# A four-layer decoder trunk on one core: weight-quarter sums spread over three layers, two more raw weight buffers and later transposes in the last layer

## The chip, the cores and the metric

The kernel runs on one core of a Trainium2 chip as one launch. The metric is the device time of that launch in microseconds (us). Each kernel is timed several times and the median is compared; the kernel before takes 844.87 us (three runs, 844.37 to 845.11).

## What is computed

Four residual layers work on x, 256 positions by 1024 channels, in float32. Layers 0 and 3 are gated MLPs with a spatial mix over chunks of 128 positions (mixer A), layer 1 is dilated-window attention (mixer B), layer 2 is causal pooling (mixer C).

```python
for i in range(DEPTH):                      # 4 layers: A, B, C, A
    h = rms_norm(x, norm_gain[i])
    x = x + mixer[i](h, ...)

def mixer_a(h, w_in, v_gain, w_s, b_s, w_out):
    proj = h @ w_in                          # 1024 x 6144
    u, v, z = proj[..., :2048], rms_norm(proj[..., 2048:4096], v_gain), proj[..., 4096:]
    mixed = einsum('gij,bcjgd->bcigd', tril(w_s), v) + b_s
    return (u * mixed * silu(z)) @ w_out     # 2048 x 1024
```

## The kernel before

**Weights as a stream.** All weights lie in DRAM as 272 units of 128 x 1024 float32 (512 KB each) in the order of their use. A unit is loaded by the SP queue into a raw buffer (tile wr, four buffers, `RAW_BUFS`), then split in two parts that the matmul takes exactly: ScalarE copies the high part (w..h, L85), VectorE subtracts to get the low part (w..l, L88). When the low part of unit u is made, the raw buffer is free and the load of unit u+4 may start. Seven pairs of split tiles exist (`W_BUFS`); a unit is split about five units before TensorE uses it (`AHEAD`). A product is three matmuls, high by high, high by low, low by high (`mm3`, L80 to L82). In most projections a unit feeds 12 matmuls with 512 columns.

**The order of the work.** The program is written by generators. A projection calls `tick()` twice per unit; each tick runs the tasks that are due (activation work, transposes, splits). `yield n` means: go on n ticks later. So the numbers in `yield` set the order of the instructions on every engine, and each engine runs its own instructions strictly in that order. SP, which issues the loads, does too: a load that has to wait holds up all loads behind it.

**The seven products.** In layer 3, the column blocks n = 1 and n = 3 of z and u are computed with seven block products in place of eight (`seven_products`, L651 to L716 of the kernel before). They need sums of weight quarters. Those sums are made during earlier layers by `sums_of_quarters` (L158): 16 rounds, each of which loads four quarters into the one tile qs (tag "xs", L167), adds four times on VectorE (L170, 128 x 256 each), and stores the result to DRAM (sums, L172). The next round's load must wait until the store has read qs. Each product unit then feeds only 6 matmuls, so units are used up twice as fast as elsewhere: 14 units in one block.

**Transposes of y.** In layers 0 and 3 a task (`y_task`, L595) multiplies u, the mixed v and the gate into yy on VectorE, then transposes yy in two halves on TensorE (yp, L620), makes high and low parts, and frees the one PSUM bank "tr" for the second half. In layer 1 the same bank takes the transposes of q and k (qt, L815), whose low parts are made at L823.

Of the kernel before, what the change touches and what calls it, by code (L numbers as in the profile page):

```python
# [10 lines left out]
F32 = mybir.dt.float32  # L11
# [6 lines left out]
P = 128  # L18
# [3 lines left out]
HALF = 512  # L22
# [15 lines left out]
RAW_BUFS = 4  # L38
# [5 lines left out]
LAST_AHEAD = 3  # L44
WARM = 13
SEVEN = (1, 3)
FIRST_PARTS = 5


@with_exitstack  # L50
def hybrid_trunk_kernel(ctx, tc, x, wts, norm_gainT, a_v_gain, a_wsT, a_bsT, b_gl, b_gv, c_scaleT,
                        masks, rope, rcnt, out):
    nc = tc.nc
    n_units = wts.shape[0]
# [42 lines left out]
    def spawn(gen, delay=0):  # L97
        if delay == 0:
            try:
                delay = next(gen)  # L100
            except StopIteration:
                return
        tasks.append([now[0] + delay, gen])
# [26 lines left out]
    used = [0]  # L130
    loaded = [0]
    split = [0]

# [11 lines left out]
                        for j in range(2)]  # L147
    n_seq = len(seq)

    def load_units(n):  # L150
        while loaded[0] < min(n, n_seq):
            i = loaded[0]
            raw = wp.tile([P, 2, HALF], F32, tag="wr", name=f"wr{i}", bufs=RAW_BUFS)
            src = sums[seq[i][0], seq[i][2]][seq[i][1]] if isinstance(seq[i], tuple) else wts[seq[i]]
            nc.sync.dma_start(raw, src.rearrange("p (k n) -> p k n", n=HALF))
            raws.append(raw)
            loaded[0] += 1

    def sums_of_quarters(parts):

        for n, j, c in parts:
            z = seven_units(n) + j
            cs = slice(c * 256, (c + 1) * 256)
            q = cp.tile([P, 4, 256], F32, tag="xs", name=f"qs{n}{j}{c}", bufs=1)
            nc.sync.dma_start(q, wts[z:z + 8:2][:, :, cs].rearrange("i p c -> p i c"))  # L167
            yield 6
            for a, b in ((0, 2), (2, 3), (3, 0), (1, 3)):
                nc.vector.tensor_tensor(q[:, a], q[:, a], q[:, b], op=ALU.add)  # L170
            yield 3
            nc.sync.dma_start(sums[n, j][:, :, cs].rearrange("i p c -> p i c"), q)  # L172
            yield 4

    lowered = [0]

    def split_hi(n):

# [8 lines left out]
    def split_units(n):  # L187

        split_hi(n)
        while lowered[0] < min(n, n_seq):  # L190
            u = lowered[0]
            lo_of(units[u][1], raws[u], units[u][0])
            lowered[0] += 1
            load_units(u + 1 + RAW_BUFS)

    def next_unit():

# [27 lines left out]


    raws.append(wp.tile([P, 2, HALF], F32, tag="wr", name="wr0", bufs=RAW_BUFS))
    loaded[0] += 1
    first_unit = wts[0].rearrange("p (k n) -> p k n", n=HALF)
    nc.scalar.dma_start(raws[0][:, 0], first_unit[:, 0])  # L230
# [20 lines left out]
    def h_parts(layer):  # L251

        o = 16 if layer in (0, DEPTH - 1) else 0
        return [hT[:, o + i * KT * S:o + (i + 1) * KT * S].rearrange("p (k s) -> p k s", s=S) for i in range(2)]
# [99 lines left out]
    def proj_first(name):  # L354

        o = [pp(f"{name}_{t}") for t in range(2)]
        pts = {}
        hh, hl = h_parts(0)

        def turn(u):  # L360
            pts[u] = (trp if u == 3 else atp)(f"hp0{u}").rearrange("p (k t c) -> p k t c", t=2, c=P)
            for t in range(2):
                for k in range(2):
                    nc.tensor.transpose(pts[u][:, k, t], xt[t][:, (2 * u + k) * P:(2 * u + k + 1) * P], ident)

        def part(k):
            return pts[k // 2][:, k % 2].rearrange("p t c -> p (t c)"), gT[:, 0, k:k + 1]

        def high(k):
            pt, g = part(k)  # L370
            nc.scalar.activation(hh[:, k], pt, AF.Copy, scale=g)

        def low(k):
            pt, g = part(k)
            nc.vector.scalar_tensor_tensor(hl[:, k], pt, g, hh[:, k].bitcast(F32), op0=ALU.mult, op1=ALU.subtract)

        def w_pair(u):
            units.append(pair(wp, [P, 2, HALF], "w", f"w{u}", W_BUFS))
            split[0] += 1

        def w_high(u, kk):
            hi_of(units[u][0][:, kk], raws[u][:, kk])

        def w_low(u, kk):
            lo_of(units[u][1][:, kk], raws[u][:, kk], units[u][0][:, kk])
            if kk:
                lowered[0] += 1
                load_units(u + 1 + RAW_BUFS)

        def products(k):  # L390

            wh, wl = (a[:, k % 2] for a in units[k // 2])
            for t in range(2):
                for i, h in enumerate(h_t(k, t)):
                    nc.tensor.matmul(o[t], h, wh, start=k == 0 and i == 0, stop=False, skip_group_check=True)
            for t in range(2):
                nc.tensor.matmul(o[t], h_t(k, t)[0], wl, start=False, stop=k == KT - 1, skip_group_check=True)

        turn(0)
        turn(1)  # L400
        w_pair(0)
        high(0)
        high(1)
        low(0)
        low(1)
        for kk in range(2):
            w_high(0, kk)
            w_low(0, kk)
        products(0)
        products(1)  # L410
        turn(2)
        high(2)
        high(3)
        low(2)
        low(3)
        w_pair(1)
        for kk in range(2):
            w_high(1, kk)
            w_low(1, kk)
        products(2)  # L420
        high(4)
        high(5)
        split_hi(3)
        low(4)
        low(5)
        split_units(3)
        products(3)
        turn(3)
        split_hi(4)
        split_units(4)  # L430
        products(4)
        high(6)
        high(7)
        low(6)
        low(7)
        for k in range(5, KT):
            products(k)
        used[0] += 4
        split_units(5)
        for t in range(2):  # L440
            ss = tiny(2, f"ss_{t}")
            for n in range(2):
                half_ss(t, n, ss)
            norm_rms(0, t, ss)
        split_units(6)
        for t in range(2):
            done.add(("h", 0, t))
        for _ in range(8):
            tick()
        return o  # L450
# [74 lines left out]

    def layer_a(layer, consts, pl, mid):
        hcur[:] = h_parts(layer)
        first = proj_first(f"v{layer}0") if layer == 0 else None
        kc, wsT, bsT = consts()

# [64 lines left out]
                mxs[n].append(mx)  # L595
            done.add(("mx", layer, n))

        def y_task(n, up, us):
            while ("mx", layer, n) not in done:
                yield 1  # L600
            yh, yl = pair(pl, [P, 4, S], "v", f"y{layer}{n}", 5)
            yT.append((yh, yl))
            ys = []
            for t in range(2):
                y = tmp("yy", f"yy{layer}{n}{t}", 2)
                if late(layer):
                    nc.vector.scalar_tensor_tensor(us[t], up[t], r_tok[t][:, 0:1], us[t], op0=ALU.mult, op1=ALU.mult)  # L607
                else:
                    nc.vector.tensor_tensor(us[t], up[t], us[t], op=ALU.mult)
                for gg in range(2):  # L610
                    sl = slice(gg * 256, (gg + 1) * 256)
                    nc.vector.scalar_tensor_tensor(y[:, sl], mxs[n][t][:, sl], bsT[:, 2 * n + gg:2 * n + gg + 1],  # L612
                                                   us[t][:, sl], op0=ALU.add, op1=ALU.mult)
                ys.append(y)
            yield 2
            for t in range(2):
                sl = slice(t * P, (t + 1) * P)
                pt = trp(f"yp{layer}{n}{t}").rearrange("p (k c) -> p k c", c=P)
                for k in range(4):
                    nc.tensor.transpose(pt[:, k], ys[t][:, k * P:(k + 1) * P], ident)  # L620
                hi_of(yh[:, :, sl], pt)
                yield 1
                lo_of(yl[:, :, sl], pt, yh[:, :, sl])
                if t == 0:
                    yield 1
            done.add(("y", layer, n))
# [24 lines left out]
        def seven_products(n):  # L651
# [41 lines left out]
            z0, u0 = r["p1"], r["n2"]  # L693
# [19 lines left out]
                yield 1  # L713

            spawn(second_task(), 1)
            spawn(y_task(n, (u0, u1), (z0, z1)), 2)  # L716

        for n in range(4):
            spawn(v_task(n, first if first and n == 0 else
# [1 line left out]
            if layer == DEPTH - 1 and n == 0:  # L721
                spawn(sums_task(), 4)
        if layer == 0:
            spawn(sums_of_quarters(parts[:FIRST_PARTS]))
        for n in range(4):
            if layer == DEPTH - 1 and n in SEVEN:
                seven_products(n)
# [39 lines left out]
    def layer_b(layer, consts, pl):  # L767
# [215 lines left out]
        for hp in range(NHEAD // 2):  # L983
            for g in range(NG):
                spawn(qk_task(hp, g, proj_tok(f"qk{hp}{g}", skew=layer if hp == 0 and g == 0 else None)))
                if hp == 0 and g == 0:
                    spawn(sums_of_quarters(parts[FIRST_PARTS:]))
                    gate(0)
                    gate(1)
            o = proj_tok(f"v01{hp}")  # L990
# [24 lines left out]
    def layer_c(layer, pl):  # L1015
# [103 lines left out]

        a, b, c, d = C_ORDER  # L1120
        spawn(gate_tok(a, proj_tok(f"cz{a}", skew=layer)))
        spawn(gate_feat(b, proj_feat(f"cz{b}")))
        spawn(pool_task(a, proj_feat(f"cx{a}")))
        spawn(pool_task(b, proj_feat(f"cx{b}")))
# [170 lines left out]
```

## Time and profile before

| | us |
|---|---|
| median of the timed runs | 844.87 |
| the profiled execution | 843.5 |
| its span on the engines | 841.7 |
| TensorE (PE) busy | 827.1 (98%) |
| VectorE (DVE) busy | 593.8 (71%) |
| ScalarE (ACT) busy | 508.5 (60%) |
| GpSimd (POOL) busy | 42.0 (5%) |

The profiled execution lies 1.4 us below the median, and the span 1.8 us below its own time. TensorE is busy nearly all the time, so what a change can win is mostly the time in which TensorE stands still, and the time in which its clock is not granted in full. Times in the rows are microseconds from the span's start. Layer 0 ends near 195 us, layer 1 near 494, layer 2 near 651.

### The profile page before, as it was taken

The page shows a single profiled execution, that of the slowest core. Times are in us where ns is not written, and L with a number is a line of the kernel's source. Part 1 is how long each engine was busy: PE and PEld are TensorE (multiplying, and loading weights), DVE is VectorE, ACT ScalarE, POOL GpSimd, SP SyncE. Part 2 cuts the span into 40 slices and gives each one's busy share as a digit, 9 for nine tenths or more (in the row PEclk, how much of TensorE's full clock was granted, in tenths as well). Part 3 has the DMA queues.
Part 4 walks back from the last instruction along what each step waited for, and adds up shares of the span by engine and source line. Part 5 has one row for each costly group of instructions (what it writes and reads, how often), then busy time and mean ns, then how long its engine had stood idle before and what let it go on. Part 6 is the DMA issues. An engine that isn't in the chain of part 4 may idle for free.

```text
span 841.7 us, 12513 instructions
## 1 busy us (share of the span) xinstructions
PE 827.1 (98%) x4565; PEld 713.0 (85%) x4565; DVE 593.8 (71%) x1006; ACT 508.5 (60%) x937; POOL 42.0 (5%) x69
## 2 busy tenths in 40 slices
PE   8998999999999999999999999999999999999998
PEld 7887888888988888888888889999988888778786
DVE  5876667546858678678668576798754898786861
ACT  7764444336768687687687567446543676565640
POOL 1101000000000010010010011000000000000000
PEclk9999999999999999999999999999999999999999
DMA  8878776662877556557566267547664467676851
GB/s 288 292 245 264 226 222 210 222 196 82 290 254 227 172 173 219 185 163 234 179 192 209 76 224 255 175 151 243 200 210 151 138 211 242 214 263 200 280 176 51
DMA packets 60654, 172.66 MB, mean 205 GB/s; under 512 B 5584, under 2 KB 22496, under 8 KB 60464
## 3 DMA queue, kind: packets, MB, share of 16 engines
q1 hardware_dynamic: 59328, 167.79, 60.6%
q0 software_dynamic: 976, 3.79, 1.4%
q8 instruction: 36, 0.59, 0.3%
q10 hardware_dynamic: 288, 0.28, 0.2%
q14 instruction: 26, 0.21, 0.1%
HBM read 162.40 MB, written 9.44 MB: 204 GB/s over the span
## 4 chain that ended last, share of the span: by engine, by line
PE 83%; DVE 7%; DMA 5%; ACT 3%; issue 2%; POOL 0%; DVEq 0%; SPq 0%; ACTq 0%
PE wo L80 6%; PE wo L82 6%; PE wo L81 6%; PE v L82 5%; PE v L80 5%; PE v L81 5%; PE qk L82 4%; PE qk L80 4%; PE qk L81 4%; PE u L81 2%; PE u L80 2%; PE u L82 2%; PE cz L81 2%; PE cz L80 2%; PE cz L82 2%
## 5 line engine op out<-in xcount | busy, mean ns | idle before, releaser
L790 POOL TENSOR_TENSOR qr<-qm,m 128x8 f32<-128x8 f32 x12 | 19.7, 1638 | 230.5 <-DVE qm L789 230.5
L785 ACT ACTIVATE junk<-qk 128x128 bf16<-128x128 f32 x96 | 26.6, 277 | 7.2 <-PE qk L82 4.5
L794 ACT ACTIVATE qn<-qk,qr 128x128 f32<-128x128 f32 x96 | 27.5, 380 | 3.4 <-POOL qr L790 3.4
L170 DVE TENSOR_TENSOR qs<-qs 128x256 f32<-128x256 f32 x64 | 27.1, 424 | 2.5 <-DMA qs<-in_wts_dram 0.9
L496 DVE TENSOR_TENSOR x<-wo,x 128x512 f32<-128x512 f32 x16 | 11.0, 689 | 20.1 <-PE wo L82 20.0
L292 ACT ACTIVATE hT<-hp,gT 128x128 fp32r<-128x128 f32 x48 | 13.0, 383 | 14.9 <-PE hp L288 14.9
L785 ACT ACTIVATION_READ_ACCUMULATOR junk<-qk 128x1 f32 x96 | 18.9, 197 | 0.0
L297 DVE SCALAR_TENSOR_TENSOR hT<-hp,gT,hT 128x128 fp32r<-128x128 f32 x48 | 13.5, 343 | 7.4 <-ACT hT L292 7.4
L274 POOL TENSOR_TENSOR r<-ms,m 128x1 f32<-128x1 f32 x6 | 4.3, 708 | 277.3 <-DVE ms L271 277.3
L789 DVE TENSOR_SCALAR qm<-qs 128x8 f32<-128x8 f32 x12 | 2.1, 172 | 22.1 <-ACT junk L785 22.1
L266 ACT ACTIVATE junk<-x 128x512 bf16<-128x512 f32 x16 | 10.2, 640 | 9.6 <-DVE x L496 9.4
L815 PE MATMUL qt<-ident,qn 128*128 128x128 f32 x96 | 14.5, 273 | 1.4 <-DVE qk10l L823 0.6
L815 PEld LDWEIGHTS qt<-ident,qn 128*128 128x128 f32 x96 | 11.3, 140 | 4.9 <-issue 2.2
L884 ACT ACTIVATE p<-p,rl 128x384 f32<-128x384 f32 (+1 forms) x16 | 11.5, 769 | 5.0 <-DVE rl L883 5.0
L620 PE MATMUL yp<-ident,yy 128*128 128x128 f32 x64 | 10.3, 285 | 4.0 <-DVE y00l L88 2.5
L620 PEld LDWEIGHTS yp<-ident,yy 128*128 128x128 f32 x64 | 7.9, 144 | 7.2 <-DVE y00l L88 2.9
L545 DVE TENSOR_TENSOR vv<-v,kc 128x512 f32<-128x512 f32 x16 | 10.7, 686 | 4.5 <-ACT junk L543 4.2
L807 DVE TENSOR_TENSOR rb<-qn,kcb 128x32 f32<-128x32 f32 x96 | 13.8, 185 | 0.0
L607 DVE SCALAR_TENSOR_TENSOR sz<-u,m,sz 128x512 f32<-128x512 f32 x8 | 6.0, 746 | 10.1 <-PE u L82 10.1
L880 ACT ACTIVATE p<-p,nb 128x768 f32<-128x768 f32 x8 | 7.5, 938 | 8.9 <-DVE nb L879 8.9
L803 DVE TENSOR_TENSOR ra<-qn,kcb 128x64 f32<-128x64 f32 x48 | 10.6, 221 | 1.0 <-ACT qn L794 0.4
L612 DVE SCALAR_TENSOR_TENSOR yy<-mx,bs,sz 128x256 f32<-128x256 f32 x24 | 10.5, 480 | 0.4
(2887 smaller groups left out, 3309.3 us busy)
## 6 DMA issues: line engine op xcount, KB each, us to landing
wr<-in_wts_dram SPq DMA_DIRECT2D x267, 512.0 KB, 4.4
qs<-in_wts_dram SPq DMA_DIRECT2D x16, 512.0 KB, 5.5
sums<-qs SPq DMA_DIRECT2D x16, 512.0 KB, 5.1
wr<-sums SPq DMA_DIRECT2D x16, 512.0 KB, 4.7
kc<-in_a_wsT_dram POOLq DMA_DIRECT2D x2, 512.0 KB, 7.4
kc<-in_a_v_gain_dram POOLq DMA_DIRECT2D x1, 1024.0 KB, 5.2
out_dram<-x SPq DMA_DIRECT2D x4, 256.0 KB, 2.0
kc<-in_a_v_gain_dram POOLq DMA_DIRECT2D x1, 768.0 KB, 6.6
```

What stands on the lines that cost most here:

```text
L80: nc.tensor.matmul(out_ap, lh[0], rh[0], start=start, stop=False, skip_group_check=True)
L81: nc.tensor.matmul(out_ap, lh[0], rh[1], start=False, stop=False, skip_group_check=True)
L82: nc.tensor.matmul(out_ap, lh[1], rh[0], start=False, stop=stop, skip_group_check=True)
L170: nc.vector.tensor_tensor(q[:, a], q[:, a], q[:, b], op=ALU.add)
L292: nc.scalar.activation(h_parts(layer)[0][:, k, t * P:(t + 1) * P], pt[:, k % 4], AF.Copy, scale=gT[:, layer, k:k + 1])
L297: nc.vector.scalar_tensor_tensor(hTl, pt[:, k % 4], gT[:, layer, k:k + 1], hTh.bitcast(F32), op0=ALU.mult, op1=ALU.subtract)
L620: nc.tensor.transpose(pt[:, k], ys[t][:, k * P:(k + 1) * P], ident)
L785: nc.scalar.activation(junk[:, :HD], ov[t][:, h], AF.Square, accum_out=ssq[t][:, h:h + 1])
L790: nc.gpsimd.tensor_tensor(rqs, ms, m05_row[:, :8], op=ALU.pow)
L794: nc.scalar.activation(qn[t][:, h], ov[t][:, h], AF.Copy, scale=rq[t][:, h:h + 1])
L807: nc.vector.tensor_tensor(rb[:, hs, s0:s0 + 16], qn[t][:, hs, s1:s1 + 16], c, op=ALU.mult)
L815: nc.tensor.transpose(pts[t][:, h], qn[t][:, h], ident)
```

## The change

The first group of rounds of quarter sums is 4 instead of 5, in layer 0; the second is 8 instead of 11, in layer 1; the remaining 4 rounds are moved to layer 2. Inside a round, the adds begin seven ticks after the load instead of six, and the four adds are one tick apart instead of together.

In layer 3, from unit 224 of the sequence on (the first unit of z), raw units go round six buffers instead of four: the four of wr, the tile xs, which the rounds no longer need by then, and a new tile wx in the layer's own pool. A load starts when the buffer it goes to is free.

In the two blocks with seven products, `y_task` waits five ticks instead of two before it transposes.

```diff
-FIRST_PARTS = 5
+PARTS = (4, 8)
...
+    raw_users = {"wr": [-1] * RAW_BUFS, "xs": [-1], "wx": [-1]}
+    last_pool = [None]
+
+    def raw_place(i):
+
+        return ("wr", "wr", "wr", "wr", "xs", "wx")[i % 6] if i >= n_units - 48 else "wr"
+
+    def load_free():
+
+        while loaded[0] < n_seq and raw_users[raw_place(loaded[0])][0] < lowered[0]:
+            load_units(loaded[0] + 1)
+
     def load_units(n):
         while loaded[0] < min(n, n_seq):
             i = loaded[0]
-            raw = wp.tile([P, 2, HALF], F32, tag="wr", name=f"wr{i}", bufs=RAW_BUFS)
+            tag = raw_place(i)
+            pool = {"wr": wp, "xs": cp, "wx": last_pool[0]}[tag]
+            raw = pool.tile([P, 2, HALF], F32, tag=tag, name=f"wr{i}", bufs=len(raw_users[tag]))
+            raw_users[tag] = raw_users[tag][1:] + [i]
...
-            yield 6
+            yield 7
             for a, b in ((0, 2), (2, 3), (3, 0), (1, 3)):
                 nc.vector.tensor_tensor(q[:, a], q[:, a], q[:, b], op=ALU.add)
-            yield 3
+                yield 1
+            yield 2
...
             lowered[0] += 1
-            load_units(u + 1 + RAW_BUFS)
+            load_free()
...
-            yield 2
+            yield wait
             for t in range(2):
                 sl = slice(t * P, (t + 1) * P)
                 pt = trp(f"yp{layer}{n}{t}").rearrange("p (k c) -> p k c", c=P)
...
-            spawn(y_task(n, (u0, u1), (z0, z1)), 2)
+            spawn(y_task(n, (u0, u1), (z0, z1), 5), 2)
...
-            spawn(sums_of_quarters(parts[:FIRST_PARTS]))
+            spawn(sums_of_quarters(parts[:PARTS[0]]))
...
-                    spawn(sums_of_quarters(parts[FIRST_PARTS:]))
+                    spawn(sums_of_quarters(parts[PARTS[0]:sum(PARTS)]))
...
         spawn(gate_tok(a, proj_tok(f"cz{a}", skew=layer)))
+        spawn(sums_of_quarters(parts[sum(PARTS):]))
```

The order on VectorE in layer 0, in the first half of the first transposed block y00; qs are the adds of a round, w29l to w32l low parts of weights. Before:

```order
62 L612 SCALAR_TENSOR_TENSOR yy_765<-mx_711,bs_254,sz_666 128x256 x2
63 L88 TENSOR_TENSOR w29l<-wr_687,w29h 128x1024
64 L170 TENSOR_TENSOR qs_727<-qs_727 128x256 x4
65 L88 TENSOR_TENSOR y00l<-yp_786,y00h 128x4x128
66 L88 TENSOR_TENSOR w30l<-wr_719,w30h 128x1024
67 L88 TENSOR_TENSOR y00l<-yp_815,y00h 128x4x128
68 L88 TENSOR_TENSOR w31l<-wr_739,w31h 128x1024
```

The same place after the change:

```order
63 L629 SCALAR_TENSOR_TENSOR yy_763<-mx_710,bs_254,sz_664 128x256 x2
64 L88 TENSOR_TENSOR w29l<-wr_686,w29h 128x1024
65 L88 TENSOR_TENSOR y00l<-yp_786,y00h 128x4x128
66 L88 TENSOR_TENSOR w30l<-wr_718,w30h 128x1024
67 L88 TENSOR_TENSOR y00l<-yp_811,y00h 128x4x128
68 L88 TENSOR_TENSOR w31l<-wr_737,w31h 128x1024
69 L186 TENSOR_TENSOR qs_775<-qs_775 128x256
70 L88 TENSOR_TENSOR w32l<-wr_755,w32h 128x1024
```

The four adds that stood ahead of both y00l now stand behind them.

The order on VectorE in layer 1, third pair of heads, from the low part of unit 117 to that of q and k (qk20l); qn is the rotation. Before:

```order
350 L808 TENSOR_TENSOR qn_3563<-ra_3655,rb_3656 128x4x32
351 L88 TENSOR_TENSOR w119l<-wr_3501,w119h 128x1024
352 L823 SCALAR_TENSOR_TENSOR qk20l<-qt_3682,gv,qk20h 128x2x128 x2
353 L88 TENSOR_TENSOR w120l<-wr_3556,w120h 128x1024
354 L170 TENSOR_TENSOR qs_3615<-qs_3615 128x256 x4
```

The same place after; two more adds stand further ahead, one between szT and yb1l and one behind w118l:

```order
367 L825 TENSOR_TENSOR qn_3544<-ra_3636,rb_3637 128x4x32
368 L186 TENSOR_TENSOR qs_3443<-qs_3443 128x256
369 L88 TENSOR_TENSOR w119l<-wr_3483,w119h 128x1024
370 L186 TENSOR_TENSOR qs_3443<-qs_3443 128x256
371 L840 SCALAR_TENSOR_TENSOR qk20l<-qt_3665,gv,qk20h 128x2x128 x2
372 L88 TENSOR_TENSOR w120l<-wr_3537,w120h 128x1024
```

Here four adds that stood behind qk20l now stand ahead of it.

The order on VectorE in layer 3 behind the first block of seven products; yy is the product that is transposed, y31l its low part. Before:

```order
759 L612 SCALAR_TENSOR_TENSOR yy_7777<-mx_7714,bs_5173,n_7734 128x256 x2
760 L88 TENSOR_TENSOR w251l<-wr_7695,w251h 128x1024
761 L88 TENSOR_TENSOR w252l<-wr_7722,w252h 128x1024
762 L88 TENSOR_TENSOR y31l<-yp_7799,y31h 128x4x128
763 L88 TENSOR_TENSOR w253l<-wr_7737,w253h 128x1024
764 L88 TENSOR_TENSOR y31l<-yp_7824,y31h 128x4x128
```

The same place after:

```order
793 L629 SCALAR_TENSOR_TENSOR yy_7781<-mx_7718,bs_5145,n_7738 128x256 x2
794 L88 TENSOR_TENSOR w251l<-wr_7673,w251h 128x1024
795 L88 TENSOR_TENSOR w252l<-wr_7685,w252h 128x1024
796 L88 TENSOR_TENSOR w253l<-wr_7699,w253h 128x1024
797 L88 TENSOR_TENSOR y31l<-yp_7830,y31h 128x4x128
798 L88 TENSOR_TENSOR w254l<-wr_7726,w254h 128x1024
799 L88 TENSOR_TENSOR y31l<-yp_7861,y31h 128x4x128
```

Each y31l stands one unit later here. On TensorE both transposes of y31 (and of y33 in the second block) stand a unit and a half further back: the first, which stood behind unit 247, is now in the middle of unit 249, the second in the middle of unit 250. On SP, the units before 224 are loaded in the same order as before between the rounds' loads and stores.

## Rows read from the trace of the kernel before

**Rows 1.** The page's list of engines: busy time, share of the span, instructions.

```profile
PE 827.1 (98%) x4565; PEld 713.0 (85%) x4565; DVE 593.8 (71%) x1006; ACT 508.5 (60%) x937; POOL 42.0 (5%) x69
```

**Rows 2.** The view of waits, TensorE alone: line, what it waited for, us in total, times, longest.

```profile
PE xb L80 <- ACT n L668: 2.5, 2, 1.5
PE yp L620 <- DVE y00l L88: 2.5, 1, 2.5
...
PE yp L620 <- DVE y31l L88: 1.1, 1, 1.1
...
PE yp L620 <- DVE y33l L88: 0.3, 1, 0.3
...
PE wo L80 <- DVE n L711: 0.3, 1, 0.3
```

**Rows 3.** The view of windows in layer 0: stretch, its length, busy us (instructions) of PE, PEld, DVE, ACT, POOL, then the granted clock, the share of the DMA engines and GB/s.

```profile
80.00:84.00 4.00, 1.58 (x7) 0.95 (x6) 3.30 (x7) 0.41 (x1) 0.00 (x0) 1.00 0.87 310
84.00:88.00 4.00, 3.91 (x13) 3.30 (x14) 3.04 (x5) 2.49 (x3) 0.00 (x0) 0.57 0.49 115
```

**Rows 4.** The timeline of TensorE there: start, us, engine, line, operation, in brackets idle time before and who ended it.

```profile
80.97 0.39 PE L81 MATMUL z<-w25l,hT 128*128 128x512 f32 x1
81.19 0.39 PE L82 MATMUL z<-w25h,hT 128*128 128x512 f32 x1
84.09 1.11 PE L620 MATMUL yp<-ident,yy 128*128 128x128 f32 x4 [2.51 <-DVE y00l L88]
...
85.43 0.63 PE L81 MATMUL z<-w26l,hT 128*128 128x512 f32 x1
85.86 0.63 PE L82 MATMUL z<-w26h,hT 128*128 128x512 f32 x1
```

**Rows 5.** The timeline of VectorE there.

```profile
79.82 1.21 DVE L88 TENSOR_TENSOR w29l<-wr,w29h 128x1024 fp32r<-128x1024 f32 x1
81.63 1.81 DVE L170 TENSOR_TENSOR qs<-qs 128x256 f32<-128x256 f32 x4 [0.60 <-DMA qs<-in_wts_dram]
83.35 0.68 DVE L88 TENSOR_TENSOR y00l<-yp,y00h 128x512 fp32r<-128x512 f32 x1
```

**Rows 6.** The timelines of SP's queue and of ScalarE there: the store of the first round, the load of the second, and the high part of unit 28.

```profile
66.66 0.43 SPq L172 DMA_DIRECT2D sums<-qs  x1
...
75.66 0.38 SPq L167 DMA_DIRECT2D qs<-in_wts_dram  x1
...
74.44 1.06 ACT L85 ACTIVATE w28h<-wr 128x1024 fp32r<-128x1024 f32 x1 [6.19 <-DMA wr<-in_wts_dram]
```

**Rows 7.** The timelines of VectorE and TensorE in layer 1, second pair of heads.

```profile
304.54 1.79 DVE L170 TENSOR_TENSOR qs<-qs 128x256 f32<-128x256 f32 x4
...
307.39 0.87 DVE L823 SCALAR_TENSOR_TENSOR qk10l<-qt,gv,qk10h 128x256 fp32r<-128x256 f32 x2
...
308.41 0.63 PE L815 MATMUL qt<-ident,qn 128*128 128x128 f32 x4 [0.56 <-DVE qk10l L823]
```

**Rows 8.** The same in the third pair of heads.

```profile
364.04 0.42 DVE L88 TENSOR_TENSOR yb1l<-szT,yb1h 128x256 fp32r<-128x256 f32 x1 [0.48 <-ACT yb1h L85]
...
369.61 0.88 DVE L823 SCALAR_TENSOR_TENSOR qk20l<-qt,gv,qk20h 128x256 fp32r<-128x256 f32 x2 [0.23 <-ACT qk20h L817]
...
371.29 0.60 PE L815 MATMUL qt<-ident,qn 128*128 128x128 f32 x4
```

**Rows 9.** The timeline of ScalarE in the two blocks of seven products.

```profile
734.65 1.06 ACT L85 ACTIVATE w245h<-wr 128x1024 fp32r<-128x1024 f32 x1 [0.17 <-DMA wr<-sums]
735.62 0.58 ACT L668 ACTIVATE n<-xb 128x512 f32<-128x512 f32 x1
...
783.47 1.06 ACT L85 ACTIVATE w267h<-wr 128x1024 fp32r<-128x1024 f32 x1 [0.20 <-DMA wr<-sums]
784.44 0.58 ACT L668 ACTIVATE n<-xb 128x512 f32<-128x512 f32 x1
```

**Rows 10.** The timeline of VectorE in the same blocks.

```profile
725.97 1.22 DVE L88 TENSOR_TENSOR w239l<-wr,w239h 128x1024 fp32r<-128x1024 f32 x1
...
774.21 1.22 DVE L88 TENSOR_TENSOR w261l<-wr,w261h 128x1024 fp32r<-128x1024 f32 x1
...
795.24 0.69 DVE L711 TENSOR_TENSOR n<-wb,n 128x512 f32<-128x512 f32 x1
```

**Rows 11.** The view of windows, columns as in rows 3: a stretch of layer 0 in which loads run one behind the other, one just before a block of seven products, and the first part of each block.

```profile
69.00:75.00 6.00, 6.00 (x32) 5.12 (x31) 0.75 (x1) 0.56 (x1) 0.00 (x0) 1.00 0.98 352
...
718.00:724.00 6.00, 6.00 (x30) 4.97 (x30) 3.86 (x7) 2.22 (x3) 0.00 (x0) 1.00 0.16 58
724.00:736.00 12.00, 11.28 (x52) 8.97 (x50) 10.00 (x11) 9.57 (x12) 0.00 (x0) 1.00 0.83 261
...
772.00:785.00 13.00, 11.52 (x54) 9.18 (x52) 10.40 (x11) 9.72 (x12) 0.00 (x0) 1.00 0.80 260
```

**Rows 12.** Layer 2: a window, and from the timelines the low part of unit 179 and the first matmul that uses it.

```profile
540.00:560.00 20.00, 20.00 (x177) 20.00 (x176) 19.73 (x31) 8.92 (x13) 0.38 (x3) 1.00 0.49 158
...
568.03 1.22 DVE L88 TENSOR_TENSOR w179l<-wr,w179h 128x1024 fp32r<-128x1024 f32 x1
...
572.58 0.28 PE L82 MATMUL cg<-cd2h,w179l 128*128 128x256 f32 x1
```

**Rows 13.** The page's list of DMA issues: KB each, median us from issue to landing.

```profile
wr<-in_wts_dram SPq DMA_DIRECT2D x267, 512.0 KB, 4.4
```

More of the change, by code (lines that the diff above doesn't have):

```diff
@@ L132, in hybrid_trunk_kernel @@
     split = [0]
+    lowered = [0]
     seq = list(range(n_units))
@@ L167, in sums_of_quarters @@
             nc.sync.dma_start(q, wts[z:z + 8:2][:, :, cs].rearrange("i p c -> p i c"))
-            yield 6
+            yield 7
             for a, b in ((0, 2), (2, 3), (3, 0), (1, 3)):
                 nc.vector.tensor_tensor(q[:, a], q[:, a], q[:, b], op=ALU.add)
-            yield 3
+                yield 1
+            yield 2
             nc.sync.dma_start(sums[n, j][:, :, cs].rearrange("i p c -> p i c"), q)
             yield 4
-    lowered = [0]
     def split_hi(n):
@@ L227, in hybrid_trunk_kernel @@
     raws.append(wp.tile([P, 2, HALF], F32, tag="wr", name="wr0", bufs=RAW_BUFS))
+    raw_users["wr"] = raw_users["wr"][1:] + [0]
     loaded[0] += 1
@@ L387, in w_low @@
                 lowered[0] += 1
-                load_units(u + 1 + RAW_BUFS)
+                load_free()
         def products(k):
@@ L527, in layer_a @@
         hcur[:] = h_parts(layer)
+        last_pool[0] = pl
         first = proj_first(f"v{layer}0") if layer == 0 else None
@@ L596, in mix_task, with y_task @@
             done.add(("mx", layer, n))
-        def y_task(n, up, us):
+        def y_task(n, up, us, wait=2):
             while ("mx", layer, n) not in done:
```

## The prediction

> **What bounds the kernel now.** I read the page's list of engines first: TensorE is busy for 827.1 of 841.7 us [rows 1], so the span can only shrink by TensorE's idle time and by time at a lower clock. Then I read TensorE's own waits [rows 2]; the reader should see that they are few and that each has a place. One wait of 2.5 us is for y00l, in layer 0. Two that add up to 2.5 us are for a ScalarE copy of xb, one in each block of seven products. y31l costs 1.1 us, y33l and L711 0.3 us each, all in layer 3. Third I read the windows around the first wait for the clock [rows 3]: from 80 to 84 us TensorE works 1.58 us at a granted clock of 1.00, and from 84 to 88 us the mean is 0.57. Last come the timelines of the engine that is waited for.
>
> A wait costs a little more than its idle time. From 81.19 to 84.09 two instructions start 2.90 us apart, where 0.22 us is the normal step from 80.97 to 81.19 [rows 4]: 2.68 us lost for 2.51 us listed idle, so I add 0.17 us per wait.
>
> **Layer 0: first round later, second round behind y00l.** The clock fell right behind the 2.51 us of idle time. Steps are 0.43 us from 85.43 to 85.86 in place of 0.22 [rows 4], which is 1.2 in place of 2.4 GHz, and a mean of 0.57 over 4 us is 1.7 us lost [rows 3]. With the pipeline's own overlap I count 1.5 us of that, so this place costs 2.7 + 1.5 = 4.2 us. Its cause is on VectorE [rows 5]: w29l is done at 81.0, the four adds then wait 0.60 us for their data and take 1.81 us, and y00l follows at 83.35. The data is late because the load of round two could not be issued before 75.66, when the store issued at 66.66 had been read out [rows 6]. In the new order the adds are behind both y00l. Without them y00l would start at 81.0 and end at 81.7, while TensorE wants the bank at 81.4: 0.3 us would be left. That rest should go too, since the store now stands behind two more weight loads on SP, which therefore start before it; unit 28, for which ScalarE stood still 6.19 us until 74.44 [rows 6], should land earlier, and with it everything that VectorE does up to w29l. Some 0.3 us earlier is enough. I take -4.2 us; the bounds are -3.8 (0.3 us left, no fall of the clock) and -4.2. What is late next there is nothing that TensorE waits for: the adds of round two come behind w31l, and weights there are split more than 5 us before use.
>
> **Layer 1: eight rounds, adds in ones and twos.** An add takes 0.45 us (1.81 for four [rows 5]). What matters is how many stand between a transpose and the low part that frees the bank. In the second pair of heads, four adds at 304.54 stand ahead of qk10l and TensorE waits 0.56 us [rows 7]; now three do, so -0.4 us. In the third pair, four adds that stood behind qk20l are now ahead of it (the order above). The first falls into an idle 0.48 us of VectorE [rows 8]; three remain, 1.35 us, less the 0.23 us for which VectorE idles before qk20l: 1.1 us later. qk20l ended at 370.49 and TensorE passed at 371.29 without a wait, with the 0.15 us that lie between the end of qk10l and the transpose that waited for it [rows 7]: slack of 0.65 us, so +0.4 us. In the other pairs as many adds stand ahead as before, or they fall where VectorE idles. The sum is 0. Bounds: -2.2 us if all waits of layer 1 went (the 0.56 us [rows 7] and the smaller ones of its kind), +2 us if three pairs were hit like the third and with no slack. The waits of up to 1.5 us did not lower the clock in this trace; the one of 2.5 us did [rows 2, 3].
>
> **Layer 2: four rounds added.** Sixteen adds of 0.45 us, 7.2 us of VectorE, beside a TensorE that never waits there; four loads and four stores on SP and the DMA engines, which are at 0.49 in the busiest stretch for VectorE [rows 12]. That stretch is the place to look at: VectorE is busy 19.73 of 20 us, and one round's 1.8 us is pushed on to the next idle time. The least slack behind it is unit 179: low part done at 569.25, first used at 572.58, 3.3 us [rows 12]. Less 1.8 us that leaves 1.5 us. I take 0; the bounds are 0 and +1 (backlog doubled by a weight load that waits behind a store on SP: 3.6 less 3.3, twice, and its refill).
>
> **Layer 3: two more raw buffers.** In each block ScalarE copies n from xb at 735.62 and 784.44, right behind the high part of a weight unit for which it had waited for a DMA [rows 9]. TensorE had finished that xb about 2.7 us before (the two units of yb, 12 matmuls of 0.227 us, come between), so the copy is late only because ScalarE's order puts it behind weights that are not there. A unit takes 1.36 us of TensorE here (6 times 0.227), a load 4.4 us [rows 13]; with the high part (1.06 us) and the low part (1.2 us) a raw buffer is tied up for about 6.8 us with its waits. Four buffers give a unit per 1.7 us, six one per 1.13 us. Just before each block the DMA engines stand at 0.16 and 58 GB/s [rows 11], for want of a free buffer: two units more can be loaded there. Worked through: unit 245's load now starts when unit 239's low part is done (727.2 [rows 10]) in place of unit 241's two units later, lands near 732, and n can follow at 733.3, done at 733.9, where TensorE wants it at 735.1 without a wait. In the second block unit 267 comes after 261 (775.4 [rows 10]), lands near 780.5, n is done at 781.7 and wanted at 783.3. Both waits go: 2.5 + 2 x 0.17 = 2.85 us. L711 (795.24 [rows 10]) then depends on VectorE, which had idled for weights before it; it ends at about 791.6 and is wanted at 791.7, so I count half of its 0.5 us. The two new buffers themselves cost nothing I can find: xs was last read by layer 3's own norm, ahead of all four v products, and the first load into it comes during the third of them.
>
> **Layer 3: later transposes.** y31l stands behind the yy products and two weight units on VectorE [rows 2]; TensorE now asks for the freed bank a unit and a half, about 4 us, later, and VectorE gets there one unit (1.2 us) later at most. So 1.1 + 0.17 = 1.3 us go, and likewise 0.5 us for y33l. Nothing waits for y31 or y33 before the output product reaches them, tens of us later.
>
> Together layer 3 offers 2.85 + 0.25 + 1.3 + 0.5 = 4.9 us. I take -4.4, since the copies' margin of 1.2 us is of the size by which a load's landing varies. Bounds: -5.1 and -1.8 (only the transposes, which need no buffer).
>
> **The sum.** -4.2 + 0 + 0 - 4.4 = -8.6 us, against the profiled execution 843.5 - 8.6 = 834.9 us. The median of the timed runs is 1.4 us above that execution, so I forecast 844.87 - 8.6 = 836.3 us.
>
> **Rivals.**
> A, transfers bind in the blocks of seven. A block takes 14 x 0.524 MB = 7.3 MB in 14 x 1.36 = 19 us, 385 GB/s, and the stretches there moved 260 GB/s [rows 11]. For: even the DMA-bound stretch in layer 0, at a share of 0.98, moved 352 GB/s. Against: the share in the blocks is 0.80 to 0.83, not 0.98, and two units lie ready in advance. If a block were fed at 300 GB/s, 1.6 MB or 3 units would be missing, two of them covered; the third costs 0.524 MB / 300 GB/s = 1.7 us per block as a wait, half of it inside lookahead: 1.8 us given back, 838.1 us. The Trainium skill (DMA: Bandwidth & Descriptors, section Bandwidth) puts the limit from HBM to SBUF at about 358 GB/s per core, below what a block asks for. This trace's 352 GB/s at a share of 0.98 fits it; by that rule alone 0.5 MB would be missing per block, which the two units cover, so the rule raises this rival's chance and not the forecast.
>
> B, a new long wait on VectorE's order in layer 1 or 2. For: adds are now scattered among low parts that free a single bank, and every engine keeps its order. Against: the slacks above. One wait like that at y00l, with the clock falling behind it, costs 4.2 us: 840.5 us.
>
> C, the wait in layer 0 stays, since the late data and not the adds set it. For: unit 28 lands late too. Against: VectorE had finished w29l 2.3 us before y00l. It would give back some 3.5 us: 839.8 us.
>
> D, slower. The four rounds in layer 2 fall on a VectorE without idle time, the loads behind their stores on SP come late, and TensorE runs out of split weights. It decides once the backlog at unit 179 passes its 3.3 us. If three rounds each cause a wait with a fall of the clock, 3 x 4.2 = 12.6 us less the 8.6 us won: 848.9 us.
>
> **How the numbers follow.** Forecast 0.70, A 0.14, B 0.07, C 0.05, D 0.04. The forecast's own range is 834 to 838. The low end of the whole range, 833.5, is every wait won: 4.2 + 5.1 + 2.2 = 11.5 us. The high end, 840.5, takes in A, B and C. A measurement of this kernel can tell about 0.2%, 1.7 us, from no change. The forecast and A, B and C are faster by more than that; D is slower, and I keep 0.03 for several of them together ending within it. So faster 0.93, same 0.03, slower 0.04.
>
> **What would show it.** Right: no wait for y00l and a granted clock of 1.00 between 80 and 90 us; no wait of xb for L668; none of yp for y31l and y33l; higher GB/s than 260 in the first part of each block and a busy DMA in the 6 us before; a wait of some 0.4 us for qk20l as a new row and a smaller one for qk10l. Wrong: any wait of 2 us or more on TensorE, a window at a clock below 1.00 before the end, or TensorE waiting at all between 500 and 650 us.

## The result, and the profile after

The changed kernel takes 833.8 us (median of four runs, 831.93 to 835.76) against 844.99 for the kernel before (median of four runs): ratio 0.9866, 95% interval 0.9841 to 0.9891, so 11.2 us or 1.3% less. Timed once more beside later experiments it took 835.6 us against 843.91, ratio 0.9896 (0.9874 to 0.9919). The forecast was 836.3 us with an own range of 834 to 838, the whole range 833.5 to 840.5.

TensorE's busy time is nearly what it was [rows 1], in a span of 831.8 us instead of 841.7. The page's list of engines of the changed kernel:

```profile
PE 825.4 (99%) x4565; PEld 713.8 (86%) x4565; DVE 590.5 (71%) x1006; ACT 507.3 (61%) x937; POOL 42.6 (5%) x69
```

All that TensorE still waits for by more than 0.15 us at a time, in the view of waits (line, what it waited for, us in total, times, longest), against [rows 2]:

```profile
PE warm L276 <- POOL m L258: 1.4, 1, 1.4
PE hp L380 <- DMA x<-in_x_dram: 0.8, 2, 0.5
PE wo L80 <- DVE cyy L1126: 0.2, 1, 0.2
```

The first two are the start, before the first product. Every row of [rows 2] is gone, and one small row in layer 2 is new: a matmul of the output projection (wo), the first of its second weight unit, 193, waits for VectorE's cyy, which frees a PSUM bank.

The windows of the changed kernel, columns as in [rows 3, 11]:

```profile
80.00:84.00 4.00, 4.00 (x23) 3.36 (x22) 2.91 (x3) 1.88 (x3) 0.00 (x0) 1.00 0.70 228
84.00:88.00 4.00, 4.00 (x19) 3.30 (x18) 3.45 (x5) 2.15 (x3) 0.00 (x0) 1.00 0.54 167
69.00:75.00 6.00, 6.00 (x34) 5.20 (x33) 2.58 (x3) 2.00 (x2) 0.00 (x0) 1.00 0.99 375
718.00:724.00 6.00, 6.00 (x32) 4.96 (x31) 5.97 (x8) 4.13 (x6) 0.00 (x0) 1.00 0.46 138
724.00:736.00 12.00, 12.00 (x60) 10.14 (x59) 11.85 (x13) 10.98 (x14) 0.00 (x0) 1.00 0.99 353
...
771.00:784.00 13.00, 13.00 (x64) 10.99 (x64) 12.41 (x13) 10.01 (x12) 0.00 (x0) 1.00 0.96 366
```

The hole in layer 0 is closed and the clock stays at 1.00 (2.4 GHz) there. In the blocks of seven products TensorE is busy throughout, and the loads run at 353 and 366 GB/s in place of 261 and 260.

**Where the time came from.** TensorE's order is fixed, so the time between the first matmuls of two units can be compared from run to run. The table has the time from the first matmul of unit 1 to that of unit 64 (layer 0), 64 to 152 (layer 1), 152 to 208 (layer 2), and from 208 to the end of the last matmul (layer 3); for the others, what is added to that of before. All are differences of starts in the timelines (the end of the last matmul for layer 3), of one profiled execution each. How far one execution may stand for others can be read off where a kernel has nothing changed against before: layer 0 of e2 and e3 (-0.59 and -1.96) and layer 3 of e1 and e4 (+0.77 and +0.75).

| us | up to unit 1 | layer 0 | layer 1 | layer 2 | layer 3 |
|---|---|---|---|---|---|
| before | 10.50 | 187.26 | 298.79 | 156.34 | 185.05 |
| changed kernel | +1.79 | -4.48 | -2.19 | +0.61 | -5.62 |
| changed kernel again (e11) | +1.60 | -4.47 | -1.81 | +2.49 | -5.62 |
| e1, rounds only | +0.02 | -4.51 | -2.20 | +0.04 | +0.77 |
| e2, buffers only | +0.29 | -0.59 | +0.05 | 0.00 | -5.62 |
| e3, later transposes only | +1.11 | -1.96 | +0.11 | +0.03 | -2.15 |
| e4, adds one tick later | +0.20 | -3.76 | +1.94 | 0.00 | +0.75 |
| e5, rounds and buffers | -0.31 | -4.47 | -2.27 | +1.45 | -5.66 |
| e6, four adds together | +1.53 | -4.48 | +0.85 | +4.51 | -5.66 |
| e7, five buffers | +0.42 | -4.47 | -2.21 | +0.04 | -4.73 |
| e8, nine rounds, more warming | +0.42 | -4.50 | -2.29 | +0.04 | -5.66 |
| e9, nine rounds | +0.18 | -4.48 | -2.17 | +0.03 | -5.66 |
| e10, more warming | +0.22 | -4.51 | -2.27 | +4.62 | -5.62 |

I take the first column for no part of the change: when the clock is first granted in full varies from profile to profile (from 4.5 us of the span on in e1, 5.5 in before, 9.5 in e3), and the two profiles of the changed kernel had it late, from 10.9 and 10.4 us on. Without it that kernel's profile would stand 11.7 us below that of before.

### The profile page after: what moved, and what is told of

Same layout as the page of the kernel before. It is cut to its first block, busy times and chain, and to the rows that moved or that the text cites. A ratio compares the mean times of both kernels' runs of the same rounds, so it can differ in the third digit from the quotient of the medians.

```text
span 831.8 us, 12513 instructions
## 1 busy us (share of the span) xinstructions
PE 825.4 (99%) x4565; PEld 713.8 (86%) x4565; DVE 590.5 (71%) x1006; ACT 507.3 (61%) x937; POOL 42.6 (5%) x69
## 4 chain that ended last, share of the span: by engine, by line
PE 89%; DVE 5%; DMA 3%; issue 1%; ACT 1%; SPq 0%; ACTq 0%; DVEq 0%
PE wo L80 6%; PE wo L82 6%; PE wo L81 6%; PE qk L82 5%; PE qk L80 5%; PE qk L81 5%; PE v L80 5%; PE v L82 5%; PE v L81 5%; PE z L82 3%; PE z L80 3%; PE u L80 3%; PE u L81 3%; PE z L81 3%; PE u L82 3%; PE qt L832 1%
## 5 line engine op out<-in xcount | busy, mean ns | idle before, releaser
L391 DVE SCALAR_TENSOR_TENSOR hT<-hp,gT,hT 128x256 fp32r<-128x256 f32 x8 | 3.5, 476 | 9.4 <-ACT hT L387 9.4
L932 PE MATMUL pt<-ident,p 128*128 128x128 f32 x48 | 9.9, 274 | 0.0
```

## The experiments

**e1 to e3: each part of the change alone.** On the changed kernel, e1 puts back four buffers and two ticks; e2 and e3 put back the old rounds and keep only the buffers, or only the five ticks.

```diff
# e1, e3
-        return ("wr", "wr", "wr", "wr", "xs", "wx")[i % 6] if i >= n_units - 48 else "wr"
+        return "wr"
# e1, e2
-            spawn(y_task(n, (u0, u1), (z0, z1), 5), 2)
+            spawn(y_task(n, (u0, u1), (z0, z1)), 2)
# e2, e3
-PARTS = (4, 8)
+PARTS = (5, 11)
...
-            yield 7
+            yield 6
             for a, b in ((0, 2), (2, 3), (3, 0), (1, 3)):
                 nc.vector.tensor_tensor(q[:, a], q[:, a], q[:, b], op=ALU.add)
-                yield 1
-            yield 2
+            yield 3
```

> The changed kernel with four raw buffers throughout and the old two ticks before y is transposed: of the change only the rounds of quarter sums are left. Theory 1 (three parts that each remove their own waits, and add up): as in the changed kernel up to layer 2, so 4.5 us less than before in layer 0, about 2 less in layer 1, 0.6 more in layer 2; in layer 3 all waits of before are back (two for L668, 2.5 us together; y31l 1.1; y33l 0.3; L711 0.3). Time 839 us. Theory 2 (the rounds in layers 0 and 1 had also delayed layer 3, through the sums): some of layer 3's waits stay away, time 835 to 837 us.

Measured: 839.74 us (837.59 to 841.62), ratio 0.9934 (0.9906 to 0.9962). Layers 0 and 1 win what they win in the changed kernel, layer 3 nothing: theory 1. The two waits for xb's copy are 3.2 us together here, where before has 2.5, which is most of the +0.77. Layer 2 shows no 0.6 us here; more on that below.

> The kernel before with six raw buffers in layer 3, and nothing else changed. Theory 1 (the buffers take away the waits for weights alone): no wait for L668 and at most half of that for L711, the wait for y31l stays near 1.1 us; 3 to 3.3 us less than before, 841.7 us. Theory 2 (VectorE gets ahead of its own queue too, so the later transposes were not needed): the waits for y31l and y33l go as well, 5 us less, 840 us. Theory 3 (transfers bind): the waits for L668 shrink by half at most, 843.5 us.

Measured: 837.63 us (836.1 to 838.02), ratio 0.991 (0.9882 to 0.9937). Layer 3 wins 5.62 us, all that the whole change wins there. TensorE's waits in e2 from layer 0 on; none is in layer 3:

```profile
PE yp L636 <- DVE y00l L88: 2.1, 1, 2.1
...
PE qt L831 <- DVE qk10l L839: 0.6, 1, 0.6
...
PE qt L831 <- DVE qk22l L839: 0.4, 1, 0.4
PE qt L831 <- DVE qk00l L839: 0.3, 1, 0.3
```

That is theory 2. The timelines of VectorE and TensorE in e2 show how:

```profile
748.63 0.68 DVE L88 TENSOR_TENSOR y31l<-yp,y31h 128x512 fp32r<-128x512 f32 x1
...
750.42 0.60 PE L636 MATMUL yp<-ident,yy 128*128 128x128 f32 x4
```

y31l is done at 749.3, and the transpose that had to wait for it in the kernel before passes at 750.42 without a wait, in its old place. VectorE had been late there because its queue held weights that were not loaded: in the first block before, up to y31l, it waits 3.7 us in all for the high parts of units 242, 243, 246 and 247, in e2 0.2 us for that of 246 alone. The longest of them, in the waits of before:

```profile
DVE w242l L88 <- ACT w242h L85: 1.2, 1, 1.2
```

> The kernel before with five ticks in place of two before the transposes of y31 and y33, and nothing else changed. Theory 1: the waits for y31l and y33l go, those for L668 stay at 2.5 us together; 1.8 us less than before, 843.1 us. Theory 2 (VectorE is late by more than four us there, so the wait moves to the next place): the waits come back at the new place of the transposes, no gain, 844.9 us.

Measured: 842.4 us (840.31 to 844.56), ratio 0.9972 (0.9952 to 0.9992). Layer 3 wins 2.15 us, the waits for L668 stay (2.6 us together). Theory 1: alone, the later transposes do work. The size is less sure, since layer 3 of e1 and e4 came out 0.8 us apart from before with no edit in it.

**e4: only the place of the adds.** In effect the kernel before with one number changed.

```diff
-            yield 6
+            yield 7
```

> The kernel before with seven ticks in place of six between a round's load and its four adds, which stay together; five and eleven rounds as before. In layer 0 the four adds then stand between the two halves of y00l instead of ahead of both. Theory 1 (the adds' place ahead of y00l made the wait of 2.5 us): no wait for y00l beyond 0.3 us and the clock stays at 1.00 there, 4.2 us less in that place. Theory 2 (the late data did: the second load behind the store and unit 28's late landing): TensorE still waits about 2 us for y00l, and the clock still falls. Elsewhere the adds move ahead of other low parts (y01l, some of q and k), which can cost 0.5 us each. Time by theory 1: 841 to 842 us, by theory 2: 845 us.

Measured: 843.51 us (841.78 to 845.84), ratio 0.9985 (0.9967 to 1.0004). The wait for y00l is gone, and both windows there are full:

```profile
80.00:84.00 4.00, 4.00 (x21) 3.27 (x21) 3.64 (x8) 2.35 (x4) 0.00 (x0) 1.00 0.77 232
84.00:88.00 4.00, 4.00 (x19) 3.32 (x18) 2.24 (x2) 1.68 (x3) 0.00 (x0) 1.00 0.60 151
```

That is what theory 1 said, with a reservation. The store's place on SP is as before in e4, and yet unit 28 landed 1.9 us earlier than in [rows 6]; why is open:

```profile
72.52 1.06 ACT L85 ACTIVATE w28h<-wr 128x1024 fp32r<-128x1024 f32 x1 [4.18 <-DMA wr<-in_wts_dram]
```

So e4 moves both things at once. Of the 2.51 us, the adds and their wait for data account for 2.3 ([rows 5], from the end of w29l to y00l); the 0.2 to 0.3 us left may have gone with the earlier landing. But the same tick puts runs of four ahead of other low parts, and TensorE's list of waits gets new rows:

```profile
PE qt L831 <- DVE qk00l L839: 0.9, 1, 0.9
...
PE qt L831 <- DVE qk20l L839: 0.6, 1, 0.6
PE o L81 <- DVE pT00l L88: 0.5, 1, 0.5
...
PE qt L831 <- DVE qk32l L839: 0.4, 1, 0.4
```

Layer 1 is 1.94 us longer than before, layer 0 keeps 3.76 of its 4.5, and no gain clear of the noise remains.

**e5: the rounds and the buffers, without the later transposes.** The second edit of e1 alone.

> The changed kernel with the old two ticks before y31 and y33 are transposed: the rounds and the two buffers are left. Theory 1 (the later transposes remove 1.8 us of their own): the waits for y31l and y33l are back, 1.1 and 0.3 us, 1.8 us more than the changed kernel. Theory 2 (after the run with the buffers alone: VectorE is early enough for both, the later transposes do nothing): no wait of either, layer 3 as long as in the changed kernel within 0.2 us, 833 to 834 us.

Measured: 833.13 us (831.6 to 837.11), ratio 0.9882 (0.9837 to 0.9927). Layer 3 is as short as in the changed kernel (-5.66 and -5.62) and TensorE waits for neither y31l nor y33l. Theory 2: beside the buffers the later transposes do nothing.

**e6: four adds together in the new places.**

```diff
             yield 7
             for a, b in ((0, 2), (2, 3), (3, 0), (1, 3)):
                 nc.vector.tensor_tensor(q[:, a], q[:, a], q[:, b], op=ALU.add)
-                yield 1
-            yield 2
+            yield 6
```

> The changed kernel with the four adds of a round in one run again, in the place where the first of them stands; rounds as long as in the change and in the same three layers. Theory 1 (an add costs VectorE 0.45 us wherever it stands): only the places where the run now stands ahead of a low part for q and k change, up to 0.5 us each at qk00l, qk10l and qk20l, and four adds in a run take 1.7 us. Theory 2 (a lone add among other work costs 0.33 us, as the changed kernel's trace shows, since only an add behind the add it reads waits for it): every low part behind a round is 0.4 us later as well. In layer 1 theory 1 gives 0.5 to 1 us more than the changed kernel, theory 2 1.5 to 2.5 us. Layer 0: no wait for y00l in either, for the run stands behind it.

Measured: 839.44 us (835.2 to 840.3), ratio 0.9929 (0.9902 to 0.9957). TensorE's waits:

```profile
PE wo L80 <- DVE cyy L1125: 2.6, 1, 2.6
PE qt L831 <- DVE qk00l L839: 1.5, 1, 1.5
...
PE qt L831 <- DVE qk10l L839: 0.6, 1, 0.6
PE qt L831 <- DVE qk12l L839: 0.4, 1, 0.4
PE qt L831 <- DVE qk22l L839: 0.3, 1, 0.3
```

Layer 1 is 3.0 us longer than in the changed kernel (0.85 + 2.19), above both theories' sizes. The 1.5 us for qk00l are a whole run of four in front of it, which I had put at 0.5 under either theory. The trace of the changed kernel shows the cheaper lone add; VectorE in the third pair of heads, and the transpose that then passes:

```profile
364.11 0.42 DVE L186 TENSOR_TENSOR qs<-qs 128x256 f32<-128x256 f32 x1
364.45 1.22 DVE L88 TENSOR_TENSOR w119l<-wr,w119h 128x1024 fp32r<-128x1024 f32 x1
365.58 0.42 DVE L186 TENSOR_TENSOR qs<-qs 128x256 f32<-128x256 f32 x1
365.92 0.87 DVE L840 SCALAR_TENSOR_TENSOR qk20l<-qt,gv,qk20h 128x256 fp32r<-128x256 f32 x2
...
366.93 0.63 PE L832 MATMUL qt<-ident,qn 128*128 128x128 f32 x4
```

The instruction behind a lone add starts 0.34 us after it, although it runs for 0.42. In [rows 5] four in a run take 1.81 us, and the next starts 1.72 us after the first, 0.43 per add: 0.46 from one add to the next, and 0.34 behind the last. Each of the last three reads what the one before wrote or overwrites what it read, and the trace has each of them waiting for a semaphore that VectorE itself raises; they start 0.03 us after the end of the add before, where y00l, which waits for none of VectorE's own, starts 0.09 us before the last add ends. No run took that wait away. Layer 2's 4.51 us is taken up under e8 to e11.

**e7: five raw buffers.**

```diff
-        return ("wr", "wr", "wr", "wr", "xs", "wx")[i % 6] if i >= n_units - 48 else "wr"
+        return ("wr", "wr", "wr", "wr", "xs")[i % 5] if i >= n_units - 48 else "wr"
```

> The changed kernel with five raw buffers in layer 3 (wr and xs, without the new tile wx). Theory 1 (a buffer is tied up for 6.8 us, so five give a unit every 1.36 us, just the pace of the blocks of seven): the waits for L668 stay under 0.5 us each, 0 to 1 us more than the changed kernel. Theory 2 (it is the number of units ready when the block begins that counts: half of the buffers, half of the gain): waits for L668 of 0.5 to 0.8 us each, and a part of the wait that L711 ends, 2 to 3 us more.

Measured: 834.86 us (832.53 to 836.33), ratio 0.9887 (0.9855 to 0.9919). One wait is left in layer 3:

```profile
PE xb L80 <- ACT n L685: 0.4, 1, 0.4
```

Layer 3 gives back 0.9 us of its 5.6. Theory 1: one more buffer brings most of it, as the pace says (6.8 us per buffer over five is 1.36 us per unit).

**e8 to e11: the wait for cyy in layer 2, and the start.** e9 has nine rounds in layer 1 and three in layer 2, e10 more warming transposes, e8 both; e11 is the changed kernel itself.

```diff
-PARTS = (4, 8)
+PARTS = (4, 9)
# e8, e10
-WARM = 13
+WARM = 16
```

> The changed kernel with nine rounds in layer 1 and three in layer 2, and 16 warming transposes at the start in place of 13. Two places: the last round's store in layer 2 no longer runs among the loads before the output product, so the 0.2 us wait for cyy goes (0.6 us with what follows it), while the ninth round stands ahead of qk32l in layer 1 and may cost 0 to 0.4 us. At the start TensorE works until x lands, so its clock should be granted in full no later than 6 us into the span, where it was at 10.9 us in the changed kernel's profile (1.8 us lost) and at 5.5 in the one of before. If the clock's first rise doesn't follow TensorE's activity there, it stays spread between 4.5 and 11 us. Time 0 to 2 us less than the changed kernel, 832 to 834 us.

> The changed kernel with nine rounds in layer 1 and three in layer 2, nothing else: the one half of the run before. If the last round's store in layer 2 makes the wait for cyy, none is left, and the high part of unit 196 waits under 1 us for its load where it waited 1.9 us in the changed kernel. If the quiet times of the run before (0.3 us apart) came from this half, these runs lie within 1 us too; 0 to 1 us less than the changed kernel's runs beside it.

> The changed kernel with 16 warming transposes in place of 13, nothing else: the other half. The wait for cyy stays (0 to 1 us). If the warming sets when the clock is first granted in full, that is at 5 to 7 us of the span and the first two weight units end 1.4 us earlier than in the changed kernel's first profile; if it doesn't, it may be anywhere between 4 and 11 us.

> The changed kernel once more, beside the two halves: no wait for L668, y00l, y31l or y33l again; a wait for cyy between 0 and 1 us; the first time of full clock between 4 and 11 us. 832 to 836 us.

Measured: e8 831.36 us (831.23 to 831.5), ratio 0.9848 (0.9824 to 0.9872); e9 831.39 us (831.2 to 831.45), ratio 0.9849 (0.9835 to 0.9864); e10 832.9 us (831.33 to 835.91), ratio 0.9872; e11 835.6 us (833.54 to 836.88), ratio 0.9896. Expectations that failed: the wait for cyy was over 1 us in both e10 and e11, e9 is 4.2 us below e11, where I had put 0 to 1, and e8 is 0.6 us below its range. The chain is in the timelines of the changed kernel, on SP, ScalarE, VectorE and TensorE:

```profile
597.10 0.43 SPq L189 DMA_DIRECT2D sums<-qs  x1
597.86 13.93 SPq L171 DMA_DIRECT2D wr<-in_wts_dram  x7
...
603.53 1.06 ACT L85 ACTIVATE w196h<-wr 128x1024 fp32r<-128x1024 f32 x1 [1.92 <-DMA wr<-in_wts_dram]
...
605.77 1.66 DVE L1126 SCALAR_TENSOR_TENSOR cyy<-cg,csc,szT 128x256 f32<-128x256 f32 x4
...
606.70 0.50 PE L80 MATMUL wo<-w193h,cy3h 128*128 128x512 f32 x1 [0.24 <-DVE cyy L1126]
```

The store of the last round is issued among the loads for the output projection. The load of unit 196 lands late, its high part waits on ScalarE, its low part holds up cyy on VectorE, and cyy holds the bank that TensorE wants. How long depends on the landing. From its issue to its landing unit 196's load takes 5.3 and 5.5 us in e1 and e7, and TensorE does not wait; 5.6 here, with a wait of 0.2; 6.0 in e5, with 1.0; and 6.8 to 6.9 in e11, e6 and e10, with 2.1, 2.6 and 2.7. The clock fell behind the last two. In e10's windows that is the mean of 0.91:

```profile
600.00:620.00 20.00, 17.28 (x77) 14.15 (x77) 12.40 (x14) 9.41 (x10) 0.00 (x0) 0.91 0.80 279
```

What makes the landing vary behind the same store is open. With that round moved to layer 1 (e8, e9) there is no store there; in e9 the load takes 4.3 us, the high part of unit 196 waits 0.27 us and cyy is not waited for:

```profile
598.29 1.06 ACT L85 ACTIVATE w196h<-wr 128x1024 fp32r<-128x1024 f32 x1 [0.27 <-DMA wr<-in_wts_dram]
```

e9's runs lie within 0.25 us of each other, and it is 1.5% faster than before; the ninth round costs nothing in layer 1 (-2.17 against -2.19). The warming is not what did it: e10 without e9's edit scatters over 4.6 us. Whether the warming brings the first full clock forward is open: it comes at 6.7 and 6.8 us of the span in the two profiles with it, later than the 6 us that I had expected of e8, and up to unit 1 they stand at +0.42 and +0.22; those without it are between -0.31 and +1.79.

## Why the prediction held, and where its steps did not

The direction was right, and the time lies in the range; but 833.8 us is just below the forecast's own 834 to 838 and 0.3 us above the low end of the whole range, and the forecast of -8.6 us was short of -11.2. That it stayed inside is in part luck: without the 0.6 us lost in layer 2, which the forecast had at 0, it would have come out below the range, as e9 does. Of the signs named, those of being right came, but for the rows for qk20l and qk10l, which are absent; of those of being wrong, TensorE waited between 500 and 650 us, for 0.2 us in the first profile and 2.1 in the second, which is also over the 2 us named. Step by step:

- **Layer 0, -4.2: right**, -4.48, in mechanism, and in size against this profile of before. Unit 28 did land earlier, as the step has it, in the changed kernel as in e4; whether that half was needed no run shows, since none has the one without the other. Rival C falls: the wait is gone. The size hangs on whether the clock falls. In e2 and e3, whose layer 0 is that of before, the wait for y00l is 2.1 and 2.0 us, and the clock falls in e2 alone (e2 above, e3 below; the granted clock is the third number from the end):

```profile
84.00:88.00 4.00, 4.00 (x14) 3.19 (x14) 3.50 (x4) 2.49 (x3) 0.00 (x0) 0.57 0.55 152
84.00:88.00 4.00, 3.15 (x16) 2.69 (x17) 3.50 (x5) 2.45 (x3) 0.00 (x0) 1.00 0.53 156
```

  Against e3's execution the same edit would win only 2.5 us in layer 0.
- **Layer 1, sum 0: this term was mis-sized.** It measured -2.2 us, the low end I had given. Two steps failed. "An add takes 0.45 us": a lone add holds VectorE for 0.34 us. With it, the three adds ahead of qk20l cost 1.0 less 0.23 us, which its slack of 0.65 nearly covers, where I had +0.4. And "in the other pairs as many adds stand ahead as before" left out most of the gain. By the steps from one matmul of TensorE to the next, qk10l gave back 0.56 us (I had 0.4), qk00l, whose four adds of before are now one, 0.53, and 1.1 us went at four more places that I had named in no term: pT00l 0.37, qk31l 0.29, qk12l and qk22l 0.24 each. Rival B falls for layer 1, where no new wait of any size came. In layer 2 it came in part: the wait for cyy is a new one on VectorE's order, and in e10, which differs from the changed kernel only in the warming, the clock fell behind it and it cost 4.6 us, about B's price.
- **Layer 2, 0: wrong.** I looked for the least slack of a weight on a busy VectorE, unit 179, whose slack fell from 3.3 to 2.1 us without a wait, and not at the last round, 25 us later, whose store meets the loads of the output projection. The cost was 0.6 us in the first profile and, beyond my bound of +1, 2.5 in the second and up to 4.6 in related kernels. It is rival D's mechanism (a store on SP ahead of weight loads) at another place and for a bank, too small to decide the sign.
- **Layer 3, buffers: right in mechanism, too small in size.** The copies of xb come on time as worked through. The changed kernel's ScalarE, against [rows 9]:

```profile
727.87 1.06 ACT L85 ACTIVATE w245h<-wr 128x1024 fp32r<-128x1024 f32 x1
728.83 0.58 ACT L685 ACTIVATE n<-xb 128x512 f32<-128x512 f32 x1
...
774.00 1.06 ACT L85 ACTIVATE w267h<-wr 128x1024 fp32r<-128x1024 f32 x1 [0.63 <-PE xb L82]
774.97 0.58 ACT L685 ACTIVATE n<-xb 128x512 f32<-128x512 f32 x1
```

  Neither unit waits for a DMA now; 1.5 us lie between the end of n at 729.4 and TensorE's first matmul into xb at 730.84. I had taken 4.4 of 4.9 us, 0.5 less for late landings; none of it was needed. In e2 TensorE's steps at the two copies are 3.1 us shorter than before (forecast 2.85); the rest of its 5.6 us are the waits for y31l (1.3) and for y33l and L711 (1.2), which I had given to the buffers for 0.25 alone.
- **Layer 3, later transposes, -1.8: right alone, wrong beside the buffers.** e3 shows 2.15 us for them alone, e5 nothing. I added two parts that remove the same lateness of VectorE. The sum stayed near only because the buffers won what I had booked to the transposes.
- **Rival A, transfers bind: it falls.** The blocks took 353 and 366 GB/s without a wait of TensorE. The limit of about 358 GB/s that the Trainium skill gives (DMA: Bandwidth & Descriptors, section Bandwidth) is not a bound here: 366 over 13 us and 375 over 6 us in layer 0 lie above it. The same section of the Trainium skill gives that figure for the case that both cores of a pair stream, and 425 GB/s as measured on a core alone, which the prediction left out. This kernel runs on one core, and its 366 and 375 GB/s lie between the two figures.

The parts alone won 5.2 us (e1), 7.3 (e2) and 2.5 (e3) by their medians, 15 together; the change won 11.2, chiefly because e2 and e3 share a gain.

## What to carry to other kernels

When one engine is busy 98% of the span, list its few waits and follow each to the queue that was late: here one queue without its data (too few raw buffers) made four rows that looked like separate causes, and a fix of the cause made the fix of a symptom superfluous. Work that is moved off the path should be followed to its last instruction, its stores too; here a store among the loads of the next stage cost a wait of nothing to 2.7 us, varying from run to run. Small dependent instructions that stand scattered can be cheaper than the same ones in a run, so price them from a row of the form that the change will have.

## What was not expected of the hardware

- A VectorE add of 128 x 256 in float32 runs 0.42 us and lets the next instruction start after 0.34 when that does not wait for it; in a run of four adds on the same quarters the step from add to add is 0.46.
- TensorE's clock fell to half (1.2 GHz) behind idle times of 2.5 us in before, 2.1 in e2, 2.6 in e6 and 2.7 in e10, but not behind 2.0 in e3 and 2.1 in e11, so around 2 us a wait can cost its own length or about 1.5 us more. At the start of e6 it also fell, from 7.7 to 11.1 us of the span, where no wait since TensorE's first matmul had been longer than 0.74 us.
